# x given transposed as well, and phase A of a hybrid decoder layer in another order: two tiles ahead of their norm, the others normalised by spread factors

## The chip, the cores and the metric

One core of one Trainium2 chip runs the kernel. The metric is the device time of one execution in microseconds. TensorE is called PE, VectorE DVE, ScalarE ACT, GpSimd POOL and SyncE SP; SP and ACT issue the DMAs.

## The reference, cut to what matters

One decoder layer on 1024 prompt rows and 64 sample rows (8 sequences of 8), width 1024. Only the parts that the change touches are spelled out:

```
h    = x * rsqrt(mean(x*x) + EPS) * norm_g          # RMSNorm, row by row
proj = h @ w_in                                     # 1024 -> 3584: q, f, i, z_a, u, v, z_b, 512 columns each
o_a  = HGRN2 recurrence(silu(q), lb + (1-lb)*sigmoid(f), i)   # lb from a softmax of lb_logits
o_a  = rmsnorm_per_head(o_a, hgrn_norm_g) * silu(z_a)
v_n  = layernorm(gelu(v)) * ln_g + ln_b
o_b  = gelu(u) * (tril(w_s) @ v_n + b_s) * silu(z_b)          # per chunk of 128 rows and head
y    = rmsnorm(x + concat(o_a, o_b) @ w_out) * final_norm_g
```

Besides y the recurrent states and the last rows of v_n are put out. All inputs are float32.

## The kernel before, in words

Each large product is made of three: operand and weight are split into a high part (rounded to the fast float32 format of PE) and a low part (the rest), and high x high, low x high and high x low are accumulated in one bank of PSUM. A bank holds 128 x 512.

Rows are cut into nine tiles: 0 to 7 of the prompt, 128 rows each, and tile 8 with the 64 sample rows. The product needs x with the model's 1024 columns on the partitions, in eight slices of K of 128. `hT` holds that for all tiles, high and low.

The program runs in stages:

- Phase A, the I projection (`i`, 512 columns). Tile after tile: load the rows (`load_x`), square and sum them on ACT (`square_x`), mean and power of -0.5 on POOL (`rsqrt_mean`, L163), scale by that factor and by `norm_g`, which lies spread over all partitions in `gB` (`scale_x`, L202, DVE), eight transposes on PE into PSUM (`turn_x`, L210), the high part by ACT (`high_x`, L219), the low part by DVE (`low_x`, L223). Then `tm_part` (L261) issues 3 matmuls for each slice of K: 24 of 128x512 for a tile, 16 for tile 8, whose high and low parts stand side by side as one operand in `hs`. `evac_i` (L289) copies the bank to `vm`; for tile 8 two DMAs fold the two halves of the bank.
- Weights come by `load_wtm` (256 KB a slice), are rounded by ACT (`high_wtm`, L252) and their rest is taken by DVE or POOL (`low_wtm`, L256).
- Phase B, the V projection, does the same with the `v` columns on the finished `hT`, then GELU, layer norm and the spatial mix (`mix`). Three small setups run beside it; two of them use PE: a transpose of twelve rows of small vectors (L378), and four of `w_s` (L400).
- Then the five other column groups head by head (`et_part`, L497), interleaved with the recurrence, and last the output product (L1274) with the final norm.

PE's instructions stand in the order of the source in the whole program. The other engines follow a scheduler's order, apart from blocks under `manual_schedule`; in phase A that block covers tile 0 and part of tile 1 on DVE and ACT. SP issues its DMAs in order; a DMA into a buffer that is still read waits, and so do all behind it. `psm` has three banks for products, `psx` three for all else.

Of the kernel before, what the change touches and what calls it, by code (L numbers as in the profile page):

```python
# [90 lines left out]
def trunk(ctx, tc, x_prompt, x_sample, state, norm_g, w_in, lb_logits, hgrn_g, ln_g, ln_b, w_s, b_s, w_out,  # L91
          final_g, consts, y_prompt, y_sample, st_prompt, st_sample, vc_prompt, vc_sample):
# [75 lines left out]
    load_x(0)  # L168
    gB = px.tile([P, D], F32, name="gB")
    nc.sync.dma_start(gB, norm_g[0].partition_broadcast(P))  # L170
    nc.sync.dma_start(idt, consts[:, 0:P])

    warm = px.tile([P, 512], F32, tag="fb", name="warm")[:, :P]
# [10 lines left out]
    warm_up(12)  # L184

    def square_x(i):
        n = tiles[i][1]
        xt = xts[i]
        xn = px.tile([P, D], F32, tag="xn", bufs=2, name=f"xn{i}")
        ss = px.tile([P, 2], F32, tag="ss", bufs=2, name=f"ss{i}")  # L190
        if i == 0:
            for b, c in enumerate(HALVES):
                S.activation(xn[:, c], xt[:, c], AF.Square, accum_out=ss[:, b:b + 1])
            V.tensor_scalar(ss[:, 0:1], ss[:, 0:1], D * EPS, None, op0=ALU.add)
            V.tensor_scalar(ss[:, 0:1], ss[:, 0:1], ss[:, 1:2], 1.0 / D, op0=ALU.add, op1=ALU.mult)
            G.tensor_tensor(ss[:, 0:1], ss[:, 0:1], half_c[:, 0:1], op=ALU.pow)
        else:
            S.activation(xn[:n], xt[:n], AF.Square, accum_out=ss[:n, 0:1])
            rsqrt_mean(ss[:n, 0:1], ss[:n, 0:1], 1, D, n)
        xts[i] = (xt, xn, ss)  # L200

    def scale_x(i, b):  # L202
# [1 line left out]
        xt, xn, ss = xts[i]
        c = slice(512 * b, 512 * b + 512)
        V.scalar_tensor_tensor(xn[:n, c], xt[:n, c], ss[:n, 0:1], gB[:n, c], op0=ALU.mult, op1=ALU.mult)

    turned_x = {}

    def turn_x(i, b):  # L210
# [1 line left out]
        xn = xts[i][1]
        ps = bank(psx, f"xps{i}_{b}")
        pv = ps.rearrange("p (k t) -> p k t", k=4)
        for k in range(4):
            PE.transpose(pv[:, k, :n], xn[:n, (4 * b + k) * P:(4 * b + k + 1) * P], idt[:n, :n])
        turned_x[i, b] = pv[:, :, :n]
# [4 lines left out]

    def low_x(i, b):  # L223
        t0, n = tiles[i]
        hi, lo = (hT[:, j, 4 * b:4 * b + 4, t0:t0 + n] for j in range(2))
        V.tensor_tensor(lo, turned_x.pop((i, b)), hi.bitcast(F32), op=ALU.subtract)
# [1133 lines left out]
```

## Time and profile before

| | |
|---|---|
| median of three runs | 532.82 us (530.58 to 533.8) |
| profiled execution | 530.24 us, its span 528.1 us |
| mean granted clock of PE | 0.994 |
| first 128x512 matmul | 11.68 us |
| phase A ends, phase B begins | 70.40 us |
| time to landing of a 256 KB weight piece, median | 5.6 us |

Times in the rows are in microseconds from the start of the span. A row of the timeline has start, duration, engine, source line, operation, output and inputs, the shape, how many instructions are merged, and in brackets the idle time before it with what ended it. A matmul's duration includes its way through the array, so matmuls overlap, and the distance between two starts is what one costs. In a table by stretch each row has the stretch, its length, busy time of PE, PE's weight loads, DVE, ACT and POOL with their counts, the granted clock, the DMA engines' busy share and GB/s. Rows of groups have busy time and mean nanoseconds, then idle time before them.

### The profile page before, as it was taken

To read this page: it belongs to the slowest core of one execution; us is meant where nothing else is said; L and a number is where in the kernel's file an instruction comes from. 1 tells how busy PE (TensorE), PEld (TensorE's weight loads), DVE (VectorE), ACT (ScalarE), POOL (GpSimd) and SP (SyncE) were. 2 spreads that over 40 slices of the span, in tenths; PEclk is the share of its full clock that TensorE was granted. 3 is DMA by queue.
4 is the path that set the end of the run, shared out by engine and by line. 5 is a ranking of instruction groups with operands and counts; after the bars stand their busy time and mean duration, and the time that the engine had idled before them with its cause. 6 is when DMAs were issued, how large, how long until landed. Compare 5 with 4: busy or idle time off the path is not lost. (4 is left out here: it accounts for less than half of the span.)

```text
span 528.1 us, 10055 instructions
## 1 busy us (share of the span) xinstructions
PE 513.7 (97%) x3821; PEld 463.4 (88%) x3821; DVE 348.7 (66%) x1113; ACT 210.9 (40%) x568; POOL 68.5 (13%) x108
## 2 busy tenths in 40 slices
PE   7899999999999999999999999999998999999995
PEld 6677877889999999999999999999997968877884
DVE  3735266777499866886769866987847775445433
ACT  5545253211136435444436435444532163223321
POOL 1411046111001101000101001001120000100010
PEclk8999999999999999999999999999999999999998
DMA  8670144000002110111002110222234383223212
GB/s 283 208 238 22 36 96 123 17 0 1 20 22 60 44 41 6 47 56 42 21 28 60 41 42 6 81 68 72 79 89 123 99 271 131 96 107 94 92 72 76
DMA packets 41192, 41.06 MB, mean 78 GB/s; under 512 B 2220, under 2 KB 32440, under 8 KB 41144
## 3 DMA queue, kind: packets, MB, share of 16 engines
q1 hardware_dynamic: 40160, 39.36, 23.7%
q10 hardware_dynamic: 984, 1.06, 0.9%
q8 instruction: 30, 0.49, 0.4%
q14 instruction: 18, 0.15, 0.1%
HBM read 32.41 MB, written 7.21 MB: 75 GB/s over the span
## 5 line engine op out<-in xcount | busy, mean ns | idle before, releaser
L1274 PE MATMUL out<-wo,mhl 128*128 128x512 f32 (+2 forms) x306 | 70.5, 383 | 0.0
L1274 PEld LDWEIGHTS out<-wo,mhl 128*128 128x128 f32 (+1 forms) x306 | 54.5, 186 | 13.6 <-DVE wo L489 0.4
L497 PE MATMUL u<-hT,wehu 128*128 128x384 f32 (+1 forms) x192 | 47.9, 332 | 0.0
L497 PE MATMUL zb<-hT,wehzb 128*128 128x384 f32 (+1 forms) x192 | 47.8, 332 | 0.0
L497 PE MATMUL f<-hT,wehf 128*128 128x384 f32 (+1 forms) x192 | 47.7, 331 | 0.0
L497 PE MATMUL q<-hT,wehq 128*128 128x384 f32 (+1 forms) x192 | 47.7, 331 | 0.0
L497 PE MATMUL za<-hT,wehza 128*128 128x384 f32 (+1 forms) x192 | 47.4, 330 | 0.0
L272 PE MATMUL tmi<-wth,hT 128*128 128x512 f32 x128 | 41.4, 404 | 0.0
L272 PE MATMUL tm<-wth,hT 128*128 128x512 f32 x128 | 40.7, 398 | 0.0
L122 DVE TENSOR_TENSOR qv<-qv,fk 128x48 f32<-128x48 f32 (+4 forms) x132 | 38.7, 320 | 0.0
L497 PEld LDWEIGHTS za<-hT,wehza 128*128 128x128 f32 x192 | 33.5, 188 | 0.7 <-issue 0.2
L497 PEld LDWEIGHTS u<-hT,wehu 128*128 128x128 f32 x192 | 33.3, 188 | 0.6
L497 PEld LDWEIGHTS zb<-hT,wehzb 128*128 128x128 f32 x192 | 33.2, 188 | 0.6
L497 PEld LDWEIGHTS f<-hT,wehf 128*128 128x128 f32 x192 | 33.3, 188 | 0.4
L497 PEld LDWEIGHTS q<-hT,wehq 128*128 128x128 f32 x192 | 33.3, 188 | 0.0
L1286 DVE TENSOR_TENSOR r<-out,xr 128x512 f32<-128x512 f32 (+2 forms) x19 | 12.5, 660 | 30.6 <-PE out L1274 30.6
L497 PE MATMUL u<-hT,welu 128*128 128x384 f32 (+1 forms) x96 | 31.4, 327 | 0.0
L497 PE MATMUL zb<-hT,welzb 128*128 128x384 f32 (+1 forms) x96 | 31.4, 327 | 0.0
L497 PE MATMUL f<-hT,welf 128*128 128x384 f32 (+1 forms) x96 | 31.4, 327 | 0.0
L497 PE MATMUL za<-hT,welza 128*128 128x384 f32 (+1 forms) x96 | 31.4, 327 | 0.0
L497 PE MATMUL q<-hT,welq 128*128 128x384 f32 (+1 forms) x96 | 31.3, 326 | 0.0
L272 PE MATMUL tmi<-wtl,hT 128*128 128x512 f32 (+1 forms) x72 | 28.7, 399 | 0.0
(255 smaller groups left out, 1158.9 us busy)
## 6 DMA issues: line engine op xcount, KB each, us to landing
wst<-in_w_in SPq DMA_DIRECT2D x16, 256.0 KB, 5.6
wos<-in_w_out SPq DMA_DIRECT2D x16, 256.0 KB, 3.7
xr<-in_x_prompt SPq DMA_DIRECT2D x8, 512.0 KB, 3.4
xt<-in_x_prompt SPq DMA_DIRECT2D x7, 512.0 KB, 4.7
out<-r SPq DMA_DIRECT2D x7, 512.0 KB, 2.6
wesf<-in_w_in SPq DMA_DIRECT2D x8, 256.0 KB, 3.0
wesq<-in_w_in SPq DMA_DIRECT2D x8, 256.0 KB, 2.9
wesu<-in_w_in SPq DMA_DIRECT2D x8, 256.0 KB, 2.9
```

What stands on the lines that cost most here:

```text
L122: eng.tensor_tensor(o, a, b, op=ALU.mult)
L272: mmul(ps[:m], lhsT=a, rhs=w, start=(k == 0 and p == 0), stop=(k == 7 and p == len(pairs) - 1), skip_group_check=i == 8)
L497: mmul(ps[:, :b - a], lhsT=wt[:, k], rhs=hT[:, j, k, a:b], start=(k == 0 and p == 0), stop=(k == 7 and p == 2))
L1274: mmul(ps[:mm, :c.stop - c.start], lhsT=a, rhs=w[:, c], start=(k == korder[0] and p == 0), stop=(k == korder[-1] and p == len(pairs) - 1), ...
L1286: V.tensor_tensor(r[:n, c], ps[:n, :w], xr[:n, c], op=ALU.add)
```

## The change

- The host lays inputs out anew, without arithmetic: `xt_prompt` and `xt_sample` hold x transposed, `gcols` has `norm_g` as columns, `cols12` the small vectors as columns, `wst_s` has `w_s` transposed. So there are no transposes on PE any more (x, L216; the twelve rows, L378; `w_s`, L400), and no `gB`.
- Tiles 0 and 1 run ahead of their norm. Their transposed columns are multiplied by `norm_g` alone: the high part on ACT for tile 0 and on POOL for tile 1, the low part on DVE (`raw_high`, `raw_low`). Their matmuls go slice by slice, six for each slice of K, as the weights arrive. The factor of each row is applied at eviction (`scale=rms[i]`).
- The other tiles are normalised in columns (`norm_x`): POOL makes a diagonal matrix of the row factors (`diag_x`), PE multiplies a matrix of ones with it (`spread_x`, 128x128 in float32), which puts the factors of all rows on every partition, and DVE multiplies column slice, `norm_g` and spread factors, eight 128x128 steps a tile, then ACT and DVE split.
- Since `hT` must hold the normalised rows for the later products, tiles 0 and 1 are loaded and normalised a second time, beside tiles 3 to 6.
- The sample tile comes third instead of fifth. It is built in `hs`, and two DMAs copy it to `hT`.
- Rows are loaded besides columns, for the sum of squares only. Some loads go to parts of `vm` that are still free.
- Phase A has a fixed order on DVE, ACT and POOL, and for the first loads on SP and ACT.
- Phase B takes the tiles in the order 8, 2 to 7, 0, 1, and its setup has two parts.

The core of the diff:

```diff
@@ RAW tiles, loads
+    RAW = (0, 1)
+    def load_cols(i, k0=0, k1=KD, by=nc.sync, place=None):
...
+        by.dma_start(xcols[i][:, k0:k1, :n], (xt_prompt[i] if i < 8 else xt_sample)[:, k0:k1])
...
-    warm_up(12)
+    warm_up(10)
+    def raw_high(i, k, eng=None):
+        t0, n = tiles[i]
+        if eng:
+            eng.tensor_scalar(hT[:, 0, k, t0:t0 + n], col(i, k)[:, :n], gcol[:, k:k + 1], None, op0=ALU.mult)
+            return
+        S.activation(hT[:, 0, k, t0:t0 + n], col(i, k)[:, :n], AF.Copy, scale=gcol[:, k:k + 1])
+    def raw_low(i, k):
+        t0, n = tiles[i]
+        hi, lo = (hT[:, j, k, t0:t0 + n] for j in range(2))
+        V.scalar_tensor_tensor(lo, col(i, k)[:, :n], gcol[:, k:k + 1], hi.bitcast(F32), op0=ALU.mult, op1=ALU.subtract)
+    def rms_x(i):
+        n = tiles[i][1]
+        ss = px.tile([P, 1], F32, name=f"ss{i}")
+        x = xrows.pop(i)[:n]
+        S.activation(x, x, AF.Square, accum_out=ss[:n])
+        rsqrt_mean(ss[:n], ss[:n], 1, D, n)
+        rms[i] = ss
+        yield
+    def diag_x(i):
+        n = tiles[i][1]
+        dg = vm[:, 5 + len(spread) % 3, 7 * P:7 * P + n]
+        G.tensor_scalar(dg[:n], idt[:n, :n], rms[i][:n], None, op0=ALU.mult)
+        spread[i] = dg
+    def spread_x(i):
+        n = tiles[i][1]
+        ps = bank(psx, f"rb{i}")[:, :n]
+        mmul(ps, lhsT=ones[:n], rhs=spread[i][:n], start=True, stop=True)
+        spread[i] = ps
     def norm_x(i):
...
+        for b in range(2):
+            c = slice(4 * b, 4 * b + 4)
+            for k in range(4 * b, 4 * b + 4):
+                V.scalar_tensor_tensor(xn[:, k], col(i, k)[:, :n], gcol[:, k:k + 1], ps, op0=ALU.mult, op1=ALU.mult)
+                yield
+            S.activation(hi[:, c], xn[:, c], AF.Copy)
+        for b in range(2):
+            c = slice(4 * b, 4 * b + 4)
+            V.tensor_tensor(lo[:, c], xn[:, c], hi[:, c].bitcast(F32), op=ALU.subtract)
+            yield
+        if i == 8:
+            for j in range(2):
+                nc.sync.dma_start(hT[:, j, :, t0:t0 + n].bitcast(F32), hs[:, :, j].bitcast(F32))
...
     def evac_i(i, ps):
+        if i in RAW:
+            S.activation(vm[:, 0:4, i * P:i * P + P], ps.rearrange("p (h e) -> p h e", h=NH), AF.Copy, scale=rms[i])
...
+    seq = [8, 2, 3, 4, 5, 6, 7]
+        fetch_wtm(I_COL, s01, (0,))
+        load_cols(0, 0, 4)
+        load_cols(1, 0, 4, nc.scalar)
...
+        for k in range(KD):
+            if k == 0:
+                high_wtm(I_COL, k)
+            raw_high(0, k)
+            if k:
+                high_wtm(I_COL, k)
+            raw_high(1, k, G)
...
+            raw_low(0, k)
+            low_wtm(I_COL, k, V)
+            raw_low(1, k)
+            tm_part(ps0, I_COL, 0, (k,))
...
+            tm_part(ps1, I_COL, 1, (k,))
...
+        makes = {2: (4,), 3: (5,), 4: (6,), 5: (7,)}
+        diags = {2: (4, 0), 3: (5,), 4: (6, 1), 5: (7,)}
+        spreads = {2: (3,), 3: (4, 0), 4: (5,), 5: (6, 1), 6: (7,)}
...
+        for a, i in enumerate(seq):
+            ps = bank(psm, f"tmi{i}")
+            tm_part(ps, I_COL, i, range(2))
+            for j in spreads.get(i, ()):
+                spread_x(j)
+            tm_part(ps, I_COL, i, range(2, KD))
...
-        PE.transpose(ps[:, :12], rows, idt[:12, :12])
-        V.tensor_copy(col12, ps[:, :12])
...
-        for h in range(NH):
-            PE.transpose(pv[:, h], ws[:, h], idt)
-        S.activation(WT, pv, AF.Copy)
...
-    vseq = [0, 1, 8, 2, 3, 4, 5, 6, 7]
+    vseq = [8, 2, 3, 4, 5, 6, 7, 0, 1]
```

How the order moves, at the places where phase A is set. First PE at the start of the program, before (`xps` are the transposes, `tmi` the banks of the I product, `wth` and `wtl` the high and low weights by slice):

```order
L182 MATMUL warmup<-warm 128x128 x12
L216 MATMUL xps_0_171<-idt,xn_163 128x128 x4
L216 MATMUL xps_1_177<-idt,xn_163 128x128 x4
L182 MATMUL warmup<-warm 128x128 x4
L272 MATMUL tmi_160<-wth_0_125,hT 128x512 x2
L272 MATMUL tmi_160<-wtl_0_126,hT 128x512
L272 MATMUL tmi_160<-wth_1_129,hT 128x512 x2
```

and now:

```order
L208 MATMUL warmup<-warm 128x128 x10
L311 MATMUL tmi_177<-wth_0_118,hT 128x512 x2
L311 MATMUL tmi_177<-wtl_0_119,hT 128x512
L311 MATMUL tmi_178<-wth_0_118,hT 128x512 x2
L311 MATMUL tmi_178<-wtl_0_119,hT 128x512
L311 MATMUL tmi_177<-wth_1_120,hT 128x512 x2
L311 MATMUL tmi_177<-wtl_1_121,hT 128x512
L311 MATMUL tmi_178<-wth_1_120,hT 128x512 x2
L311 MATMUL tmi_178<-wtl_1_121,hT 128x512
```

The transposes of tile 0 and the four warm-up calls behind them are gone, and each slice of K now has the matmuls of tile 0 (`tmi_177`) and of tile 1 (`tmi_178`) before the next slice of weights is needed.

Next DVE at the start, before:

```order
L194 TENSOR_SCALAR ss_164<-ss_164 128x1
L195 TENSOR_SCALAR ss_164<-ss_164 128x1
L206 SCALAR_TENSOR_TENSOR xn_163<-xt_99,ss_164,gB 128x512 x2
L258 TENSOR_TENSOR wtl_0_126<-wst_0_123,wth_0_125 128x512
L226 TENSOR_TENSOR hT<-xps_0_171,hT 128x4x128
L258 TENSOR_TENSOR wtl_1_130<-wst_1_127,wth_1_129 128x512
L226 TENSOR_TENSOR hT<-xps_1_177,hT 128x4x128
L258 TENSOR_TENSOR wtl_2_134<-wst_2_131,wth_2_133 128x512
L258 TENSOR_TENSOR wtl_4_144<-wst_4_141,wth_4_143 128x512
```

and now (`xc_125` and `xc_127` are the columns of tiles 0 and 1):

```order
L222 SCALAR_TENSOR_TENSOR hT<-xc_125,gcol,hT 128x128
L297 TENSOR_TENSOR wtl_0_119<-wst_0_117,wth_0_118 128x512
L222 SCALAR_TENSOR_TENSOR hT<-xc_127,gcol,hT 128x128
L222 SCALAR_TENSOR_TENSOR hT<-xc_125,gcol,hT 128x128
L297 TENSOR_TENSOR wtl_1_121<-wst_0_117,wth_1_120 128x512
L222 SCALAR_TENSOR_TENSOR hT<-xc_127,gcol,hT 128x128
L222 SCALAR_TENSOR_TENSOR hT<-xc_125,gcol,hT 128x128
L297 TENSOR_TENSOR wtl_2_132<-wst_2_130,wth_2_131 128x512
L222 SCALAR_TENSOR_TENSOR hT<-xc_127,gcol,hT 128x128
```

The sums, the scaling of the rows and the reading of transposes from PSUM (`xps`) are gone. Each slice of K has two low parts of 128x128 and one low part of weights; all eight weight slices are DVE's, where POOL had three.

Last PE in the middle of a tile, before (tile 1):

```order
L272 MATMUL tmi_271<-wth_3_137,hT 128x512 x2
L272 MATMUL tmi_271<-wtl_3_138,hT 128x512
L216 MATMUL xps_0_284<-idt,xn_253 128x128 x4
L216 MATMUL xps_1_291<-idt,xn_253 128x128 x4
L272 MATMUL tmi_271<-wth_4_143,hT 128x512 x2
L272 MATMUL tmi_271<-wtl_4_144,hT 128x512
```

and now (tile 3, `rb` are the spread factors):

```order
L311 MATMUL tmi_408<-wth_1_120,hT 128x512 x2
L311 MATMUL tmi_408<-wtl_1_121,hT 128x512
L253 MATMUL rb_415<-vm 128x128
L253 MATMUL rb_417<-vm 128x128
L311 MATMUL tmi_408<-wth_2_131,hT 128x512 x2
L311 MATMUL tmi_408<-wtl_2_132,hT 128x512
```

In place of eight transposes for the next tile stands one product with the matrix of ones, or two where a tile is normalised for the second time.

More of the change, by code (lines that the diff above doesn't have):

```diff
@@ L166, in rsqrt_mean @@
         G.tensor_tensor(out, out, half_c[:rows, :n_cols], op=ALU.pow)
[L168 to L173, printed above, removed]
+    gcol = keep.tile([P, KD], F32, name="gcol")
+    nc.scalar.dma_start(gcol, gcols)
+    warm = px.tile([P, D], F32, tag="xs", bufs=2, name="warm")[:, :P]
     V.memset(warm, 0.0)
@@ L202, in scale_x @@
-    def scale_x(i, b):
-        n = tiles[i][1]
[L204 to L210, printed above, removed]
-        n = tiles[i][1]
[L212 to L217, printed above, removed]
@@ new lines, in trunk, with load_wtm, fetch_wtm @@
+    wparts = {}
+    def load_wtm(col, ks, place):
+        st = place[0].tile([P, KD, P], F32, tag=place[1], name=f"wst{col}_{ks[0]}").rearrange("p k e -> p (k e)").rearrange(
+            "p (j c) -> p j c", j=2)
+        for k in ks:
+            hi = wtm.tile([P, 512], F32R, tag="wth", name=f"wth{col}_{k}")
+            lo = wtm.tile([P, 512], F32R, tag="wtl", name=f"wtl{col}_{k}")
+            wparts[col, k] = (hi, lo, st[:, k % 2])
+        return st
+    def fetch_wtm(col, st, ks, by=nc.sync):
+        src = win[ks[0] * P:(ks[-1] + 1) * P, col:col + 512].rearrange("(j p) c -> p j c", p=P)
+        by.dma_start(st[:, ks[0] % 2:ks[0] % 2 + len(ks)], src)
@@ L342, in trunk @@
[L342 to L357 removed]
+            t = px.tile([P, 2, 512], F32, tag="xs", bufs=2, name="ifold")
@@ new lines, in evac_i @@
+            folded(t[:, 0], t[:, 1], ps)
+            fold.append(lambda: V.tensor_tensor(vis, t[:, 0], t[:, 1], op=ALU.add))
+    seq = [8, 2, 3, 4, 5, 6, 7]
+    places = [(we, "weh")] * 3 + [(we, "wel")] * 3
+    s01 = load_wtm(I_COL, (0, 1), places[0])
+    with tc.manual_schedule(engines={mybir.EngineType.Activation, mybir.EngineType.SP}):
+        fetch_wtm(I_COL, s01, (0,))
+        load_cols(0, 0, 4)
+        load_cols(1, 0, 4, nc.scalar)
+        fetch_wtm(I_COL, s01, (1,))
+        fetch_wtm(I_COL, load_wtm(I_COL, (2, 3), places[1]), (2, 3))
+        load_cols(0, 4, KD)
+        load_cols(1, 4, KD)
+        S.activation(lb, half_c[:, 0:NH], AF.Sigmoid)
+        load_rows(8)
+        fetch_wtm(I_COL, load_wtm(I_COL, (4, 5), places[2]), (4, 5))
+        nc.sync.dma_start(idt, consts[:, 0:P])
+        xcols[8] = px.tile([P, KD, P], F32, tag="xs", bufs=2, name="xc8")
+        load_cols(8)
+        fetch_wtm(I_COL, load_wtm(I_COL, (6, 7), places[3]), (6, 7))
+        load_rows(2)
+        load_cols(2)
+        load_rows(0, place=2)
+        load_rows(3)
+        load_cols(3, place=1)
+        load_rows(1, place=3)
+        nc.sync.dma_start(cst, consts[:, P:])
+        nc.sync.dma_start(col12, cols12)
+        load_rows(4)
+        load_cols(4, place=2)
@@ L417, in evac_v @@
         if i == 8:
-            fa, fb = folded(pv_, ps, "vfold", ("fa", 1, "fb", 1))
+            fa, fb = (pv_.tile([P, 512], F32, name=f"vfold{j}") for j in range(2))
+            folded(fa, fb, ps)
             src = fb[:n]
```

251 lines of the change are left out of this document (116 added, 135 removed).

## The prediction

> **What bounds the kernel now.** I read the page's table of engines first, then a table of busy time by stretch, then PE's own timeline through phase A (the I projection), where the change works.
>
> ```profile
> PE 513.7 (97%) x3821; PEld 463.4 (88%) x3821; DVE 348.7 (66%) x1113; ACT 210.9 (40%) x568; POOL 68.5 (13%) x108
> ...
> 0.00:11.60 11.60, 8.26 (x39) 7.78 (x40) 4.12 (x11) 5.69 (x12) 0.76 (x5) 0.92 0.78 268
> 11.60:70.40 58.80, 56.74 (x276) 45.51 (x274) 30.13 (x43) 29.84 (x57) 12.28 (x21) 0.99 0.41 129
> 70.40:130.00 59.60, 59.60 (x288) 48.67 (x287) 42.60 (x82) 15.96 (x28) 17.28 (x24) 1.00 0.17 47
> 130.00:528.10 398.10, 389.10 (x3224) 361.49 (x3222) 271.83 (x979) 159.37 (x474) 38.17 (x59) 1.00 0.22 69
> ```
>
> PE is busy from end to end: this is a chain of matmuls, and time is saved only by removing work from PE, or by starting it sooner. DVE has about half its time free between 11.6 and 70.4, ACT too. Next, what PE does there:
>
> ```profile
> 1.04 5.45 PE L182 MATMUL warmup<-warm 128*128 128x128 f32 x24 [1.04 <-DVE euler L176]
> 8.78 1.54 PE L216 MATMUL xps<-idt,xn 128*128 128x128 f32 x8 [2.29 <-DVE xn L206]
> ...
> 11.68 1.20 PE L272 MATMUL tmi<-wth,hT 128*128 128x512 f32 x2
> ...
> 15.70 0.40 PE L272 MATMUL tmi<-wtl,hT 128*128 128x512 f32 x1
> 17.06 0.66 PE L216 MATMUL xps<-idt,xn 128*128 128x128 f32 x4 [0.96 <-DVE xn L206]
> 18.82 0.63 PE L216 MATMUL xps<-idt,xn 128*128 128x128 f32 x4 [1.10 <-DVE xn L206]
> 19.20 0.72 PE L272 MATMUL tmi<-wth,hT 128*128 128x512 f32 x2
> ...
> 23.96 0.39 PE L272 MATMUL tmi<-wtl,hT 128*128 128x512 f32 x1
> 24.20 1.03 PE L216 MATMUL xps<-idt,xn 128*128 128x128 f32 x8
> 24.99 0.72 PE L272 MATMUL tmi<-wth,hT 128*128 128x512 f32 x2
> ...
> 70.17 0.39 PE L272 MATMUL tmi<-wtl,hT 128*128 128x512 f32 x1
> 70.40 0.63 PE L272 MATMUL tm<-wth,hT 128*128 128x512 f32 x2
> ```
>
> From 70.17 to 70.40 one 128x512 matmul takes 0.233 us: a tile of 128 rows (24 matmuls) takes 5.6 us, the sample tile (16) takes 3.73. All nine are 48.5 us, but phase A ends at 70.40. The rest is: no matmul before 11.68; a stall of tile 0 from 15.94 to 19.20 behind the transposes of tile 1; and eight transposes in each later tile, 0.79 us from 24.20 to 24.99.
>
> As a check of this accounting: 19.20 to 70.40 is 51.2 us. Nine matmuls of tile 0 (2.1), seven tiles (39.2), the sample tile (3.7) and seven sets of transposes (six of 0.79, about 0.7 for the sample's) make 50.4. The 0.8 left over, 0.1 a tile, I carry into the sum for after.
>
> **The change part by part.** *Removed from PE:* all 72 transposes of x, and in phase B two small sets:
>
> ```profile
> 75.77 0.40 PE L272 MATMUL tm<-wtl,hT 128*128 128x512 f32 x1
> 76.09 0.23 PE L378 MATMUL ps<-idt,rows 12*128 12x12 f32 x1
> 76.25 0.74 PE L272 MATMUL tm<-wth,hT 128*128 128x512 f32 x2
> ...
> 81.73 0.39 PE L272 MATMUL tm<-wtl,hT 128*128 128x512 f32 x1
> 81.96 0.60 PE L400 MATMUL psw<-idt,ws 128*128 128x128 f32 x4
> 82.32 0.48 PE L272 MATMUL tm<-wth,hs 128*128 128x512 f32 x1
> ```
>
> From 75.77 to 76.25 is 0.48, less one matmul of 0.233: 0.25 us. From 81.73 to 82.32 is 0.59, less one: 0.36. Phase B saves 0.6.
>
> *Added on PE:* nine float32 products with the matrix of ones, 128x128. The nearest rows are four float32 mixes of that size (two records each):
>
> ```profile
> 92.03 1.16 PE L451 MATMUL mix<-WT,vg 128*128 128x128 f32 x8
> 92.94 0.72 PE L272 MATMUL tm<-wth,hT 128*128 128x512 f32 x2
> ```
>
> 0.91 us for four: 0.23 each. Two fall before the sample tile, seven after it: 1.6 us.
>
> *The start.* The first matmul no longer waits for a norm, a scaling and a transpose. It needs a 256 KB piece of weights, half of tile 0's columns, and a conversion on ACT. The rows that price this:
>
> ```profile
> 3.42 0.63 ACT L193 ACTIVATE xn<-xt 128x512 f32<-128x512 f32 x1 [1.19 <-DMA xt<-in_x_prompt]
> ...
> L254 ACT ACTIVATE wth<-wst x8: 615/624/632, 8.8 to 14.8; 128x512 fp32r<-128x512 f32 x8
> L898 ACT ACTIVATE on<-o,oss 128x128 f32<-128x128 f32 x32 | 9.6, 366 | 7.7 <-POOL oss L166 7.7
> ```
>
> Today's first load, of the same 256 KB, has landed at 3.42, the second about 1.1 later. So weights are at hand at 3.4, columns at 4.5 (up to 5.3, since a third load shares the engines), and 0.62 and 0.37 of ACT give the first operands at 4.9 to 5.7. The warm-up is ten calls instead of twelve: 1.04 + 5.45 x 10/12 = 5.6. First matmul at 5.6 instead of 11.68.
>
> From there six matmuls a slice of K, 1.4 us, are 11.2 us, if fed. The last weights decide. Ahead of them and with them 3.74 MB stand in the queue (weights 2.10, columns 1.05, sample 0.52, identity 0.07); today the same 3.74 MB (weights 2.10, x0 and x1 1.05, the spread gain 0.52, identity 0.07) have landed when the last conversion starts at 14.8. So slice 6 begins near 14.3, is converted by 14.9, and then DVE has two slices left. DVE's rows:
>
> ```profile
> 404.95 2.15 DVE L1072 SCALAR_TENSOR_TENSOR s<-s,s_a,s_u 128x128 f32<-128x128 f32 x8
> 25.51 1.28 DVE L226 TENSOR_TENSOR hT<-xps,hT 128x512 fp32r<-128x512 f32 x2
> 24.18 1.42 DVE L206 SCALAR_TENSOR_TENSOR xn<-xt,ss,gB 128x512 f32<-128x512 f32 x2 [1.83 <-POOL ss L166]
> 15.24 3.43 DVE L206 SCALAR_TENSOR_TENSOR xn<-xt,ss,gB 128x512 f32<-128x512 f32 x2 [0.72 <-POOL ss L166]
> ```
>
> Eight 128x128 scalar_tensor_tensor in 2.15 are 0.26 apart; 128x512 subtractions come 0.6 apart. A slice is 2 x 0.26 + 0.61 = 1.13 on DVE, under PE's 1.4, plus four 128x64 steps of the sample's norm (0.21 each, an estimate from the 0.26) after slices 5 and 6. From 14.9: 0.61 + 0.26 + 0.84 + 1.13 = 17.75, and PE finishes at 18.0.
>
> The last row holds the cost that I can't place exactly. The same pair of operations takes 3.43 us at 15.24 and 1.42 at 24.18. Beside the first one GpSimd was at work:
>
> ```profile
> 13.83 0.75 POOL L165 TENSOR_SCALAR ss<-ss 128x1 f32<-128x1 f32 x1
> 15.18 2.95 POOL L258 TENSOR_TENSOR wtl<-wst,wth 128x512 fp32r<-128x512 f32 x2
> 19.47 0.19 POOL L165 TENSOR_SCALAR ss<-ss 128x1 f32<-128x1 f32 x1 [1.35 <-ACT xn L198]
> L122 POOL TENSOR_TENSOR qm<-s_q,cst 128x128 f32<-128x128 f32 x8 | 3.5, 474 | 2.5 <-PE s_sc L1056 1.8 <-ACT s_q L943 0.7
> ```
>
> The two engines keep each other out. The change gives GpSimd eight scalings of 128x128 (tile 1's high parts), in two bursts of four, in the very stretch where DVE subtracts. One costs between 0.19 (128x1, alone) and 0.47 (128x128 with two inputs); I take 0.33, the middle, 2.65 us in all. The first burst falls where DVE waits for weights, the second where it doesn't: 1.3 us. The sample tile then starts at 18.0 + 1.3 + 0.23 = 19.5. Bounds: 17.3 (5.6 + 11.2 + two products of 0.23) and 22.0 (18.0 + 8 x 0.47 + 0.23).
>
> *The steady part.* A norm is now eight 128x128 steps and two subtractions on DVE, 8 x 0.26 + 2 x 0.61 = 3.3 us. Tiles 0 and 1 are normalised a second time, beside tiles 3 to 6. Eight norms of 3.3 are 26 us under 35 us of PE, and the fullest tile carries 3.3 + 1.0 + 1.2 = 5.5 of 5.8. I cost it at nothing; what it costs if that cover goes is a rival below. ACT has two halves of 0.6, a square of 1.25 and an eviction of 0.6 a tile: 3.1 of 5.8.
>
> *The loads.* x comes twice (rows for the norm, columns for the product), and tiles 0 and 1 have their columns loaded again. Tile 4's columns must be in near 30.7; 8.3 MB stand up to them.
>
> ```profile
> 10.00:12.50 2.50, 2.50 (x12) 2.40 (x11) 2.50 (x5) 2.49 (x6) 0.31 (x1) 0.50 1.04 393
> 12.50:15.00 2.50, 2.50 (x10) 1.95 (x10) 0.78 (x2) 2.50 (x6) 2.33 (x3) 0.87 1.04 401
> ...
> 20.00:22.50 2.50, 2.50 (x12) 2.04 (x11) 2.01 (x3) 0.98 (x3) 0.30 (x1) 1.00 0.97 244
> ```
>
> Today 11.6 x 268 plus 3.4 x about 397 make 4.46 MB by 15.0. The other 3.83 MB take 9.8 us at 390 GB/s (in at 24.8), 15.7 at 244 (30.7, just in time). SP issues in order and stands behind ACT's eviction of the sample tile (its fold) before it asks for the last rows and columns; that is near 29, with 12 us to go before tile 6 needs them.
>
> *The sum.* Phase A ends at 19.5 + 3.73 + 6 x 5.6 + 1.6 + 0.8 = 59.2 instead of 70.40: 11.2, with phase B's 0.6 it is 11.8. Behind that nothing is moved. The span goes from 528.1 to 516.3. The profiled execution took 530.24, under the three runs shown (median 532.82); what lies around the span stays. I set the saving against the median: 532.8 - 11.8 = **521.0**.
>
> [...] The row at 10.00 shows a granted clock of 0.50, and 0.87 behind it, after a hole of only 2.3 us (6.5 to 8.78): 2.5 x 0.50 + 2.5 x 0.13 = 1.6 us of PE lost. After the change PE is fed piece by piece from 5.6 on, with holes that I put under 1.5 us, and I take no loss. [...]
>
> **The rivals.**
>
> *A crawling start (0.18).* GpSimd's scalings at 0.47 each, all visible on DVE (2.5 over my start), and one clock drop (1.6): 521.0 + 4.1 = 525.1. For it: the 3.43 row and the 0.50. Against: DVE waits for weights in the first half anyway. [...]
>
> *Loads late (0.09).* Up to and with the V weights 15.4 MB must land (the 8.3 above, 4.2 for tiles 5 to 7 and the two reloads, 0.8 of copies of the sample tile, 2.1 of weights); 4.46 are in by 15.0, and 10.9 remain. At 244 GB/s they take 45 us, to 60, which is about when they are used. At half of today's 390, as short pieces (1 KB and 256 bytes) might make it, they take 56, to 71: the whole head start is gone, about 531. Against: at 390 it is 28 us, to 43.
>
> *DVE becomes the bound (0.05).* If the 128x128 step that reads the spread factors from PSUM cost far more than 0.26, the norms would set the pace: eight of 8s + 1.21 against 35.2 us. From s = 0.39 they decide; from 0.57 the change loses. At 0.75, what the 128x512 step costs, they are 57.7: 22.5 more, 532.8 - 11.8 + 22.5 = 543.5. Against: the row with 0.26 also reads PSUM.
>
> **How the numbers follow.** The forecast has 0.68. The best start (17.3) gives 518.8, and a run's scatter of 1 us or so 517.5; the crawling start 525.1, with scatter 526.0. The range 517.5 to 526.0 holds both, less their tails, about 0.8. A measurement tells about 1%, 5.3 us: faster 0.86 (forecast and crawl), same 0.09, slower 0.05.
>
> **What would show it.** First 128x512 matmul near 5.6; the sample tile's near 19.5; phase B's first near 59; DVE's 128x128 steps 0.26 apart; no idle time of PE between tiles. I am wrong if DVE's steps come 0.4 apart, if PE waits for loads after 25 us, or if stages behind phase B grow.

## The result, and the profile after

The change takes the median from 532.73 us (530.58 to 533.8, four runs) to **518.96 us** (518.77 to 519.61, four runs): a ratio of 0.9749 with a 95% interval of 0.9717 to 0.978. 521.0 was predicted, 517.5 to 526.0 as the range. The total is close, but one large term was wrong, and others made up for it. The profiled execution took 519.07, its span 517.3.

| us | before | before, profiled again | after | predicted |
|---|---|---|---|---|
| first 128x512 product | 11.68 | 12.27 | 5.80 | 5.6 |
| start of the sample tile (end of the two-tile start) | - | - | 24.02 | 19.5 |
| phase B begins | 70.40 | 72.44 | 63.06 | 59.2 |
| length of phase B, to the first product of `f` | 55.38 | 55.38 | 54.37 | 54.8 |
| `f` to the first product of `z_a` | 233.38 | 233.38 | 233.45 | 233.4 |
| `z_a` to the first output product | 63.29 | 65.18 | 61.63 | 63.3 |
| output product to the end | 105.65 | 105.92 | 104.79 | 105.65 |

PE's timeline after, in the columns known from before:

```profile
5.80 0.90 PE L311 MATMUL tmi<-wth,hT 128*128 128x512 f32 x2 [0.47 <-ACT hT L217]
...
11.89 0.40 PE L311 MATMUL tmi<-wtl,hT 128*128 128x512 f32 x1
14.36 0.73 PE L311 MATMUL tmi<-wth,hT 128*128 128x512 f32 x2 [2.08 <-ACT wth L293]
...
23.88 0.39 PE L253 MATMUL rb<-vm 128*128 128x128 f32 x2
24.02 0.48 PE L311 MATMUL tmi<-wth,hs 128*128 128x512 f32 x1
...
63.06 0.40 PE L311 MATMUL tm<-wth,hs 128*128 128x512 f32 x1
```

The start ran to 12.1 with one gap of 0.19 us, then PE waited 2.08 us for the conversion of the fifth slice of weights (k = 4). From 24.02 on there is no idle time up to phase B. The table by stretch, same columns as before (granted clock, DMA share and GB/s last):

```profile
7.50:10.00 2.50, 2.50 (x12) 2.03 (x11) 2.37 (x7) 1.45 (x3) 1.60 (x2) 1.00 1.08 257
10.00:12.50 2.50, 2.28 (x10) 1.50 (x8) 0.84 (x2) 0.15 (x1) 0.00 (x0) 1.00 1.04 226
12.50:15.00 2.50, 0.64 (x2) 0.30 (x2) 1.02 (x2) 2.50 (x6) 1.24 (x3) 1.00 1.16 317
15.00:17.50 2.50, 2.50 (x7) 1.67 (x7) 1.57 (x4) 1.04 (x3) 2.50 (x5) 0.51 1.03 407
17.50:20.00 2.50, 2.50 (x7) 1.93 (x6) 2.50 (x10) 1.08 (x3) 0.71 (x1) 0.50 1.06 373
20.00:22.50 2.50, 2.50 (x9) 1.98 (x8) 2.50 (x10) 2.50 (x7) 1.15 (x2) 0.62 1.07 356
```

Two things stand out. Between 7.5 and 12.5 us the DMA engines are busy throughout (share above 1) and move only 257 and 226 GB/s, where they move 356 to 407 later. And behind the hole the clock is 0.51, 0.50 and 0.62: of 7.5 us, 3.4 are lost. What the other engines did then:

```profile
12.35 1.06 ACT L236 ACTIVATE xt<-xt 64x1024 f32<-64x1024 f32 x1 [2.80 <-DMA xt<-in_x_sample]
15.32 2.88 POOL L215 TENSOR_SCALAR hT<-xc,gcol 128x128 fp32r<-128x128 f32 x4
15.96 1.18 DVE L222 SCALAR_TENSOR_TENSOR hT<-xc,gcol,hT 128x128 fp32r<-128x128 f32 x2 [0.93 <-POOL hT L215]
16.30 0.63 ACT L293 ACTIVATE wth<-wst 128x512 fp32r<-128x512 f32 x1 [0.89 <-DMA wst<-in_w_in]
...
21.83 0.75 DVE L269 TENSOR_TENSOR hs<-xn,hs 128x256 fp32r<-128x256 f32 x2
L215 POOL TENSOR_SCALAR hT<-xc,gcol x8: 593/688/1181, 5.8 to 17.1; 128x128 fp32r<-128x128 f32 x8
```

ACT stood 2.80 us in front of the square of the sample's rows (tile 8), which had not landed; the conversions for k = 4 stand behind it. POOL makes the factors and the diagonal from that square, and only then tile 1's scalings of k = 4 to 7, 0.69 us each (last row: minimum, median and maximum in ns). DVE waits for the first of them, and then works without a gap from 15.96 to 22.6. The weights of k = 6 were in only at 16.30. From this I had three suspects for the lost 4.5 us: small pieces that slow the loads, ACT in order behind the rows, and the clock.

### The profile page after: what moved, and what is told of

Its sections match the earlier page's. It is cut to its first block, busy times and chain, and to the rows that moved or that the text cites. A ratio compares the mean times of both kernels' runs of the same rounds, so it can differ in the third digit from the quotient of the medians.

```text
span 517.3 us, 10015 instructions
## 1 busy us (share of the span) xinstructions
PE 506.2 (98%) x3750; PEld 456.6 (88%) x3750; DVE 359.8 (70%) x1184; ACT 211.7 (41%) x569; POOL 78.6 (15%) x123
## 5 line engine op out<-in xcount | busy, mean ns | idle before, releaser
L311 PE MATMUL tmi<-wth,hT 128*128 128x512 f32 x128 | 43.0, 418 | 2.5 <-ACT wth L293 2.1
L311 PEld LDWEIGHTS tmi<-wth,hT 128*128 128x128 f32 x128 | 24.7, 198 | 9.3 <-ACT wth L293 2.5
L1359 DVE TENSOR_TENSOR r<-out,xr 128x512 f32<-128x512 f32 (+2 forms) x19 | 12.5, 660 | 29.2 <-PE out L1347 29.2
```

Of the source, the lines that this page charges most:

```text
L311: mmul(ps[:m], lhsT=a, rhs=w, start=(k == 0 and p == 0), stop=(k == 7 and p == len(pairs) - 1), skip_group_check=i == 8)
L1359: V.tensor_tensor(r[:n, c], ps[:n, :w], xr[:n, c], op=ALU.add)
```

## The experiments

Each kernel but the repeat of before is the changed kernel with the edit shown; experiment 10 takes over the edit of 9, and 11 that of 10. A measured time is the median of its executions; in brackets stand its ratio to the kernel before and the 95% interval of the ratio. "Start" is the start of the sample tile, 24.02 after the change. Lines left out of an edit are marked with three dots.

**1. The sample's transposed x packed.**

```diff
-        xcols[8] = px.tile([P, KD, P], F32, tag="xs", bufs=2, name="xc8")
+        xc8 = px.tile([P, KD, P], F32, tag="xs", bufs=2, name="xc8")
+        xcols[8] = xc8.rearrange("p k t -> p (k t)")[:, :KD * NS].rearrange("p (k t) -> p k t", k=KD)
```

> The sample tile's transposed x is stored packed, so its 256 KB load goes in rows of 2 KB instead of pieces of 256 B; nothing else changes. Small pieces (theory): they are what lowered the rate to 226 to 257 GB/s in 7.5 to 12.5 us at a full DMA share, so the rows of tile 8 land about 1.5 us sooner (12.35 now), the hole before the weight part k = 4 shrinks from 2.1 to 0.6 us or less, the clock is not lowered, and the sample tile starts at 19.5 to 20.5 instead of 24.0: 3.5 to 4.5 us less in all. Bytes alone (rival): the same bytes stand ahead of the same loads, so the hole stays at about 2 us, the start at 24, and the time within 0.3 us. Shut gate alone (second rival: the clock would be lowered whatever the hole): the hole shrinks but the clock row still shows 0.5, and the gain is 1.5 us at most.

Measured: 519.25 us (0.9754, 0.9737 to 0.9771), start 23.89. The packets under 512 bytes between 5 and 15 us fell from 1164 to 143, and the rate between 7.5 and 12.5 us was still 281 and 220 GB/s. The small pieces of the sample's columns are not the cause. The hole was gone, because PE came to it later (first product at 6.52, clock 0.51 between 7.5 and 10), and that gained nothing.

**2. The square of the sample's rows one slice later.**

```diff
-            if k == 3:
+            if k == 4:
                 list(rms_x(8))
                 diag_x(8)
```

(and `spread_x(8)` at k = 5 instead of 4.)

> ScalarE's square over the sample's rows stands one weight part later (behind the conversion of k = 4 instead of k = 3), with its diagonal and its spread; the loads are untouched. In-order wait (theory): ScalarE stood behind the late rows of tile 8, not behind weights, so the conversion of k = 4 moves from 13.69 to when its weights land; if they landed by 12, the hole goes from 2.1 to 0.5 us or less and the sample tile starts at 20 to 21, 3 to 4 us less. Late transfers (rival): the weights of k = 4 land as late as the rows, the hole stays above 1.5 us, and the time moves by less than 0.7 us.

Measured: 519.2 us (0.975, 0.9731 to 0.9768), start 23.77: the rival. ACT, now free to take the weights first, waits for them just as long:

```profile
13.11 0.63 ACT L293 ACTIVATE wth<-wst 128x512 fp32r<-128x512 f32 x1 [3.15 <-DMA wst<-in_w_in]
```

The weights of k = 4 land only at 13.1. They stand behind the rows in the same queue (after the change the rows are asked for at 4.07 us, these weights at 4.67), and both are late.

**3. TensorE kept busy through the hole.**

```diff
+            if k == 4:
+                warm_up(8)
             tm_part(ps0, I_COL, 0, (k,))
```

> Eight extra 128x128 products of zeros into the unused warm-up bank stand on TensorE ahead of the weight part k = 4, that is in the hole of 2.1 us; no load and no other engine changes. Clock (theory): the hole is what lowers the granted clock to 0.5 from 15 to 22 us, and it cost about 3.4 us; with TensorE busy through the hole the clock rows stay at 1.00, the hole itself stays (k = 4 still begins near 14.4), and the sample tile starts at about 20.5, 3 to 3.5 us less. No gate (rival): the clock falls anyway, or the feed of k = 5 to 7 (weights converted at 14.5, 16.3, 19.5) sets the pace in its place: the gain is under 1.5 us.

Measured: 519.03 us (0.9748, 0.9733 to 0.9763), start 23.34. The clock did stay up, and the start came 0.7 us sooner. But the sample's rows landed 0.7 us sooner in this run as well (ACT's square begins at 11.64 instead of 12.35), so nothing is left that the clock must have given: the rival. The table by stretch, then ACT, DVE and PE of this run:

```profile
15.00:17.50 2.50, 2.50 (x10) 1.46 (x10) 2.24 (x5) 0.63 (x1) 2.50 (x4) 1.00 1.02 396
17.50:20.00 2.50, 2.39 (x10) 1.48 (x9) 2.50 (x11) 1.76 (x4) 0.03 (x1) 1.00 1.06 376
```

```profile
11.64 1.06 ACT L236 ACTIVATE xt<-xt 64x1024 f32<-64x1024 f32 x1 [2.25 <-DMA xt<-in_x_sample]
15.26 1.20 DVE L222 SCALAR_TENSOR_TENSOR hT<-xc,gcol,hT 128x128 fp32r<-128x128 f32 x2 [0.93 <-POOL hT L215]
...
21.15 0.75 DVE L269 TENSOR_TENSOR hs<-xn,hs 128x256 fp32r<-128x256 f32 x2
23.10 0.49 PE L253 MATMUL rb<-vm 128*128 128x128 f32 x2 [0.88 <-POOL vm L246]
```

Here is the long link: DVE has 6.6 us of work without a gap from 15.26 to 21.9 (seven low parts of x, three of weights, eight steps of the sample's norm and its two subtractions), and PE follows piece by piece. Then PE waits 0.88 us for the diagonal of tile 2, whose spread stands ahead of the sample tile; POOL makes it behind ACT's square of tile 2, which stands in ACT's list behind work that waits for DVE. The same wait ends the start in experiments 1, 2, 5, 6 and 8 (0.70 to 0.89 us). After the change, at half clock, PE had no gap in that stretch and came to the spread at 23.88, when the diagonal had been done since 23.72: two limits of about equal length, of which taking one away shows nothing.

**4. Tile 1's scalings on ScalarE.**

```diff
-            raw_high(1, k, G)
+            raw_high(1, k)
```

> Tile 1's eight raw scalings in the start are ScalarE's (as tile 0's are) instead of GpSimd's; nothing else changes. Theory (a chain from the late rows of tile 8: square on ScalarE, factor and diagonal on GpSimd, then GpSimd's raw scalings of k = 4 to 7, then VectorE's list, which runs without a gap from about 15.3 to 21.9 in the runs with a full clock): one link goes, VectorE's wait of 0.93 us for GpSimd ends, and the first tile after the two starts 0.5 to 1 us sooner, if ScalarE's eight more scalings (0.3 each behind one another) don't eat it. Rival (late weights decide): the weights of k = 6 and 7 land at about 15.5 whatever GpSimd does, the start is where it was, within 0.3 us of 23.9, and so is the time.

Measured: 519.17 us (0.9735, 0.9678 to 0.9793), start 23.57, no gain that can be told. But the rows landed later in this run, and behind them the chain is shorter:

```profile
13.26 1.06 ACT L236 ACTIVATE xt<-xt 64x1024 f32<-64x1024 f32 x1 [1.58 <-DMA xt<-in_x_sample]
```

From the square's begin to the start are 10.3 us here. After the change they are 11.7 (12.35 to 24.02), in experiment 1 as well (12.19 to 23.89) and in experiment 3 (11.64 to 23.34), with quite different clocks. That the distance stays the same while its ends move by 0.7 us is the best evidence for the chain, and it is 1.4 us shorter without POOL's scalings. This is one profile, and PE, at half clock for part of the time (0.994 in the mean of this run), had no gap from 15.27 on; the end of DVE's work, which stands before PE, came 1.6 us nearer to the square (8.6 us behind its begin, 10.2 after the change).

**5. The sample's rows asked for sooner.** `load_rows(8)` and the identity stand right behind the weights of k = 2 and 3.

```diff
         fetch_wtm(I_COL, load_wtm(I_COL, (2, 3), places[1]), (2, 3))
+        load_rows(8)
+        nc.sync.dma_start(idt, consts[:, 0:P])
         load_cols(0, 4, KD)
         load_cols(1, 4, KD)
...
-        load_rows(8)
...
-        nc.sync.dma_start(idt, consts[:, 0:P])
```

> The sample's rows (and the identity) are asked for right behind the weights of k = 2 and 3, ahead of the second halves of tile 0's and 1's transposed x, so 0.5 MB sooner in the queue; bytes and engines' lists are the same. Theory (the chain that begins at the late rows): the rows land 1 to 1.5 us sooner than 12.2, GpSimd's diagonal and its scalings of k = 4 to 7 follow, VectorE's unbroken stretch begins 0.5 to 1 us sooner, and the sample tile starts at 22.8 to 23.3: 0.5 to 1.2 us less in all. Rival (weights of k = 4 to 7 landing at about 13.1 and 15.5 decide): the start stays within 0.3 us of 23.9. It also shows whether the stretch of 115 to 230 GB/s between 8.5 and 11.5 us moves to an earlier time with these rows (a transfer into 64 partitions only) or stays where it is.

Measured: 518.35 us (0.973, 0.9684 to 0.9777), start 22.90, phase B at 61.93. The first experiment in which the start moves as the chain from the rows says, by 1.1 us, although the first product came late in this run (7.19):

```profile
10.05 0.63 ACT L293 ACTIVATE wth<-wst 128x512 fp32r<-128x512 f32 x1 [1.61 <-DMA wst<-in_w_in]
11.40 1.04 ACT L236 ACTIVATE xt<-xt 64x1024 f32<-64x1024 f32 x1
22.90 0.48 PE L311 MATMUL tmi<-wth,hs 128*128 128x512 f32 x1
```

From the square to the start are 11.5 us. ACT now waits for weights ahead of the square and no longer for the rows themselves. In the whole time the interval doesn't tell it from the change. The slow stretch moved too: 198 GB/s between 7.5 and 10 us, 347 between 10 and 12.5. It goes where the sample's rows go.

**6. The sample's rows over all partitions.** What is special about them: 64 rows fill 64 partitions. This kernel leaves half of each row out of the sample's sums.

```diff
+        if i == 8:
+            nc.sync.dma_start(xrows[i][:, :512], src.rearrange("t (c d) -> (t c) d", c=2))
+            return
         nc.sync.dma_start(xrows[i][:n], src)
...
+        m = n if i < 8 else P
+        x = xrows.pop(i)[:m] if i < 8 else xrows.pop(i)[:, :512]
```

> The changed kernel with the sample's rows loaded as 128 half rows of 2 KB into 128 partitions instead of 64 rows of 4 KB into 64; the sample's factors are then computed from wrong sums (half a row), so this part of the result is left out, and ScalarE's square is 0.4 us shorter. Theory (a transfer into 64 partitions only is what holds the rate at 115 to 230 GB/s between 8.5 and 11.3 us): the stretch goes, the windows of 7.5 to 12.5 us show 330 GB/s or more instead of 257 and 226, the rows land 1 to 1.5 us sooner and so do the weights behind them (k = 6's conversion at 14.5 to 15 instead of 15.5 to 16.3). Rival (the rate is low there for another reason, such as the source of the second halves of the transposed x): the stretch stays, with rates within 10% of 257 and 226.

Measured (one execution): 517.6 us, span 515.8; start 21.55, phase B at 60.59, 2.5 us sooner than after the change. The stretch and ACT:

```profile
7.50:10.00 2.50, 2.48 (x6) 2.00 (x7) 2.50 (x7) 1.57 (x4) 2.50 (x3) 0.50 1.06 404
10.00:12.50 2.50, 2.50 (x11) 2.00 (x10) 1.77 (x6) 1.81 (x5) 1.47 (x4) 0.82 1.17 301
```

```profile
10.29 0.63 ACT L240 ACTIVATE xt<-xt 128x512 f32<-128x512 f32 x1 [0.59 <-DMA xt<-in_x_sample]
14.44 0.63 ACT L297 ACTIVATE wth<-wst 128x512 fp32r<-128x512 f32 x1 [0.99 <-DMA wst<-in_w_in]
```

404 GB/s instead of 257 (and 301 instead of 226, where 330 or more was expected), the rows 2.1 us sooner, the weights of k = 6 at 14.4 instead of 16.3. The same 256 KB into 64 partitions held up all that stood behind it. The edit also halves the pieces, from 4 KB to 2 KB, and no run takes the two apart. Against the length of the pieces speaks the profile after the change: the rows of tile 2, pieces of 4 KB too but for 128 partitions, were asked for at 8.3 us and landed 9.2 us later, at the end of the stretch with 407 GB/s. The stretches of 2.5 us hold other loads too; from 8.5 to 11.5 us after the change 162 GB/s were moved at a full share (1.04). Why a load into 64 partitions should be slower is shown by no run. From the square to the start are 11.3 us, 11.7 less the 0.4 by which the square is shorter: the same chain, begun sooner. The clock was 0.50 between 7.5 and 10 us, which cost nothing that shows. Of the 2.5 us the span shows 1.5 (515.8 against 517.3): the stretch from the output product to the end took 105.60 here and 104.79 after the change.

**7. The two tiles taken apart**, to price the idea of the start: tile 1's products all behind tile 0's.

```diff
-            tm_part(ps1, I_COL, 1, (k,))
             if k == 7:
+                tm_part(ps1, I_COL, 1, range(KD))
                 spread_x(2)
```

> The two-tile start taken apart: in the start TensorE does only tile 0's products with each weight part as it comes; tile 1's 24 products stand behind tile 0's last ones. Loads and the other engines' lists are the same (the sample's spread stays behind k = 4). Theory (the start is set by a chain on the other engines that ends at about 22 us, and TensorE fills its waits with tile 1): tile 1's 24 products (0.234 us each, 5.6 us) now stand behind that end, apart from the 0.7 to 0.9 us that TensorE waits there anyway: the sample tile starts at 27 to 29 us instead of 24.0 and the time is 3.5 to 5 us longer. Rival (TensorE sets the pace of the start): the same products in another order cost nothing, within 0.5 us.

Measured: 524.15 us (0.9849, 0.9831 to 0.9868), 5.2 us over the change (the profiled execution 4.1):

```profile
14.15 0.74 PE L311 MATMUL tmi<-wth,hT 128*128 128x512 f32 x2 [2.72 <-ACT wth L293]
...
28.07 0.48 PE L311 MATMUL tmi<-wth,hs 128*128 128x512 f32 x1
```

The start ends 4.05 us later. So of the 5.6 us of tile 1's products in the start some 4 lay in waits of PE, at much the same clock (0.67, 0.50 and 0.50 here in the stretches from 15 to 22.5 us, 0.51, 0.50 and 0.62 after the change).

**8. Transposes put back**, eight of the identity behind each spread of tiles 3 to 7, 0 and 1.

```diff
+        if i not in (8, 2):
+            jk = bank(pss, f"jk{i}")
+            for h in range(8):
+                PE.transpose(jk[:, h % 4 * P:h % 4 * P + P], idt, idt)
```

> Eight transposes of the 128x128 identity into an unused bank stand behind each spread of tiles 3 to 7, 0 and 1: 56 of the kind that the change took off TensorE (eight took 0.79 us before), with no reader. Theory (TensorE sets the pace in the steady part): phase B starts 7 x 0.79 = 5.5 us later, and the time is 5 to 5.8 us longer. Rival (TensorE waits there for VectorE's and ScalarE's normalisation anyway, so the transposes were covered): under 1 us.

Measured: 525.91 us (0.9875, 0.9826 to 0.9924), 6.95 over the change, more than the 5 to 5.8 expected:

```profile
23.50 0.48 PE L315 MATMUL tmi<-wth,hs 128*128 128x512 f32 x1
...
29.10 1.04 PE L258 MATMUL jk<-idt 128*128 128x128 f32 x8
...
68.76 0.40 PE L315 MATMUL tm<-wth,hs 128*128 128x512 f32 x1
```

From the start to phase B are 45.26 us instead of 39.04: 6.2 for seven sets, 0.89 each. (The start came 0.5 us sooner, and 1.3 us of the rest lie behind phase B.) The steady part was PE's, and each set of transposes cost its full time there.

**9. All links at once.** Rows early as in 5; raw scalings and low parts of k = 4 to 7 ahead of the late weights; the sample's norm in one piece; tile 2's square and spread inside the sample tile.

```diff
+            if k == 3:
+                list(rms_x(8))
+                diag_x(8)
+                for j in (4, 5):
+                    raw_high(0, j)
+                    raw_high(1, j)
+                    raw_low(0, j)
+                    raw_low(1, j)
...
             if k == 5:
-                norm8 = norm_x(8)
...
+                list(norm_x(8))
```

> All links of the start's chain at once: rows of tile 8 early as in the run with early rows; the raw scalings and their low parts for k = 4 to 7 ahead of the late weights' conversions, in VectorE's hole of 2 us (six of the eight highs on ScalarE, two on GpSimd behind the diagonal); the sample's normalisation in one piece between the weights of k = 5 and 6, so ScalarE does not stand before it; tile 2's square, diagonal and spread behind the start, inside the sample tile. Theory: VectorE has 6.7 us of work from about 12.2, so the sample tile starts at 19 to 20.5 instead of 24, 3.5 to 5 us less, and the time is 514 to 515.5. Rival (the weights of k = 6 and 7, landed at 15.5, are the wall): TensorE still has twelve products of k = 6 and 7 and the rest of k = 5 behind them, and with conversions the start is not below 19; if they land later still, the gain is under 2 us. Second rival: tile 2 is then late and gives 1 us or more back before it.

Measured: 519.59 us (0.9754, 0.97 to 0.9808). The start is 2.5 us sooner, not the 3.5 to 5 expected, and tile 2 (27.89 after the change) gives 1.5 of it back, the second rival:

```profile
21.50 0.39 PE L311 MATMUL tmi<-wth,hs 128*128 128x512 f32 x1
...
26.89 0.50 PE L311 MATMUL tmi<-wth,hT 128*128 128x512 f32 x1 [1.30 <-ACT vm L329]
```

**10. The same, mended at its waits.**

```diff
-    ps0, ps1 = bank(psm, "tmi0"), bank(psm, "tmi1")
+    ps0, ps1 = bank(psm, "tmi0"), bank(pss, "tmi1")
...
+            if k == 6:
+                high_wtm(I_COL, 6)
+                high_wtm(I_COL, 7)
```

> The run with all links at once, mended at its three new waits: the sample's spread ahead of k = 4's products instead of between them, both conversions of k = 6 and 7 ahead of ScalarE's copies of the normalised sample, and tile 1's sums in a bank that is otherwise empty here, so tile 2 does not wait for tile 0's eviction (1.30 us in that run). Theory (the start's end is the end of a chain of links, each of which is the next to decide): the sample tile starts at 19.8 to 20.8, tile 2 follows it without the 1.3 us of wait, phase B starts at 59.5 to 60.8 instead of 62.3 to 63.1, and the time is 516 to 517: 2 to 3 us less than the changed kernel. Rival (what is saved ahead of the sample tile is given back at tile 2 and 3, whose rows come later than TensorE then wants them): phase B still starts at 62 or later and the time is within 1 us of 519.

Measured: 518.97 us (0.9754, 0.9733 to 0.9774). Start at 20.12 and tile 2 at 24.04, as the theory said; phase B at 62.10, as the rival said:

```profile
20.12 0.39 PE L311 MATMUL tmi<-wth,hs 128*128 128x512 f32 x1
...
24.04 0.40 PE L311 MATMUL tmi<-wth,hT 128*128 128x512 f32 x1
36.55 1.06 ACT L236 ACTIVATE xt<-xt 128x1024 f32<-128x1024 f32 x1 [5.85 <-DMA xt<-in_x_prompt]
38.27 0.49 PE L311 MATMUL tmi<-wth,hT 128*128 128x512 f32 x1 [1.54 <-ACT hT L266]
```

Of the 3.9 us gained at the start 2.9 are lost before phase B, some 2.2 of them at tile 4 and 0.5 at tile 2: ACT stands 5.85 us before the rows of tile 5, and the copies of tile 4, which PE wants, stand behind it in ACT's order. These rows did not come sooner with the start: they were asked for at 30.72 (30.43 after the change) and landed 5.8 us later in both. After the change ACT stood before them too, for 3.10 us up to 36.22, which PE did not feel. The transfers run at a full share (1.00 to 1.08 in all stretches of 5 us from 20 to 40), and each tile now needs x twice; that this is what keeps the request back was not tested.

**11. With wide rows and the copies ahead of the squares.** Besides, the halves of the sample's rows are added by the spread, its transposed x is packed as in 1, and rows are asked for one tile sooner.

```diff
+            V.tensor_scalar(rb, ps, EPS, None, op0=ALU.add)
+            G.tensor_tensor(rb, rb, half_c[:, 0:1].to_broadcast([P, NS]), op=ALU.pow)
...
+            if new:
+                list(norm_x(new[0]))
             for j in makes.get(i, ()):
                 list(rms_x(j))
...
-            if new:
-                list(norm_x(new[0]))
```

> The version that the runs point to: the mended start, and the three things that still held it. The sample's rows come as 128 half rows into all partitions (as in the run with wide rows) with the right sums: the halves are added by the spread itself through a 128x64 matrix of pairs, and the power is taken on the 128x64 result, one GpSimd operation that no earlier trace shows on this shape. The sample's transposed x is packed. In the steady part ScalarE copies the tile that TensorE wants next before it squares the rows of the tile after it, and those rows are asked for ahead of tile 0's second load. Theory (after the start, phase A is paced by transfers at a full DMA share until about 50 us, and by ScalarE standing in order behind late rows): the sample tile starts at 18.5 to 19.8 us, no tile behind it waits over 0.5 us, phase B starts at 58.8 to 60.3 instead of 62 to 63, and the time is 515 to 516.5: 2.5 to 4 us less than the changed kernel. Rival (the transfers alone decide: 10 MB in phase A end when they end): phase B starts at 60.5 to 61.5 and the time is 517 to 518. Second rival: the power on 128x64 takes 3 us or more, the sample's columns wait for it, and the start is back at 22 or later.

Measured: 529.84 us (0.995, 0.9927 to 0.9972): the second rival, and far beyond it.

```profile
13.01 10.94 POOL L272 TENSOR_TENSOR rb<-rb,half_c 128x64 f32<-128x64 f32 x1 [0.95 <-DVE rb L271]
26.45 0.80 PE L333 MATMUL tmi<-wtl,hT 128*128 128x512 f32 x1 [9.83 <-DVE wtl L319]
```

The wide rows did their part, this time with whole rows in the sums:

```profile
7.50:10.00 2.50, 2.50 (x12) 2.06 (x11) 2.45 (x7) 2.04 (x5) 1.83 (x3) 1.00 1.05 398
10.00:12.50 2.50, 2.50 (x13) 2.05 (x11) 2.50 (x10) 2.50 (x10) 0.73 (x1) 1.00 1.06 391
```

But the power on 128x64 took 10.94 us; on 128x1 it takes 0.57. From these two shapes I estimate 0.16 us for each further column, so the factors should be made before they are spread. A version with whole sums made before the spread wasn't tried, so no run here is a finished kernel that beats the change by more than the measurement can tell.

**12. The kernel before, profiled again.**

> The kernel before, unchanged, profiled once more. If the 1.7 us that the change gained between z's last part and the output stage (wait for the state's load 1.9 us before, 0.3 after) is chance in the landing of a store, this profile shows a wait other than 1.9 us, or one as long as before with the same landings; if it belongs to the kernel, the wait is 1.7 to 2.1 again. The stretch from output to end (105.7 before, 104.8 after) likewise: 105.5 to 105.9 if it is the kernel's. The span should lie between 528 and 531.

Measured: 534.44 us, span 532.3, over the expected range. PE's wait for the state's load was 2.33 us, 1.90 in the first profile and 0.28 after the change. The rows of before again, then of after:

```profile
411.72 2.14 PE L1056 MATMUL s_sc<-s,qm 128*32 128x128 f32 x30 [2.33 <-DMA s<-in_state_hgrn]
...
411.00:417.00 6.00, 5.28 (x43) 4.61 (x44) 1.96 (x7) 0.00 (x0) 0.00 (x0) 0.72 0.27 82
...
out<-s SPq DMA_DIRECT2D x8, 256.0 KB, 3.5
```

```profile
399.34 1.28 PE L1131 MATMUL s_sc<-s,qm 128*32 128x128 f32 x30 [0.28 <-DMA s<-in_state_hgrn]
...
out<-s SPq DMA_DIRECT2D x8, 256.0 KB, 2.4
```

The wait is outside the 1.7 to 2.1 us that were to show a property of the kernel, so this run alone does not settle it. But in all twelve profiles of the changed kernel and its variants the wait is 0.3 to 0.7 us, and in both of before 1.9 or more, so I take it for a property of the program and not for chance. The load waits on SP for an earlier store of the state to land (last rows: issues, size, median us to landing), and that takes 3.5 us in both profiles of before, 2.4 after. Why the same store lands sooner in the changed program was not tested and stays open. In this run the hole of 2.33 us was followed by a clock of 0.72; behind the 1.90 of the first profile the clock stayed at 1.00. That accounts for 1.5 us of the difference between the two profiles of before.

## Why the prediction was right, and where it was wrong

**The first product, 5.6: right.** 5.80; over the twelve kernels it is 5.8 to 7.2, set by when the first columns land.

**The start, 19.5 with bounds of 17.3 and 22.0: wrong, 24.02.** The step that failed is "the last weights decide", with DVE's two last slices behind them from 14.9. The weights of k = 6 came 2.0 us later (16.3 instead of 14.3), and DVE then had more than two slices left: from 15.96 it worked 6.6 us without a gap. GpSimd's scalings were undersized one by one, 0.69 us instead of 0.33 and above my upper bound of 0.47, but experiment 4 puts them at some 1.4 us of the path, where the sum had 1.3; they are not where the 4.5 us went. What the sum lacked was the chain that starts at the sample's rows: 256 KB into 64 partitions, at 257 and 226 GB/s between 7.5 and 12.5 us, hold up the rows and all weights behind them; ACT's square, POOL's diagonal and POOL's scalings come in order behind that; DVE's 6.6 us follow, and behind DVE come PE and the diagonal of tile 2, which the sum left out as well. I had set 3.74 MB after against 3.74 MB before; the bytes are the same, but before, these rows stood far behind the first weights. Experiment 6 mends it at its head: 2.5 us, in one execution.

The rival of the crawling start put this point at 19.5 + 4.1 = 23.6, the nearest number of all, by scalings at 0.47 and one clock drop. The scalings were dearer and the drop came, but the number is near by luck: experiment 4 leaves the scalings near what the forecast had, and in experiment 3, with the clock at 1.00, the start came no sooner than its rows, where the clock rows show 3.4 us as lost. A half clock on an engine that waits for its feed cost little here.

**The steady part: right in its numbers, wrong in one reason.** From the start to phase B it is 39.04 against my 39.7; the spreads took about 0.15 instead of 0.23, the DVE steps came 0.26 to 0.27 apart, and no idle time of PE stands between the tiles. Experiment 8 shows that PE sets the pace there. The loads were priced by tile 4's columns, "in at 24.8 to 30.7, just in time". What I did not price are the rows of tile 5: ACT stands in order before them, and tile 4's copies stand behind them. After the change that was covered only because the start was late; with the start at 20.12, experiment 10 waits at tile 4, and phase B begins at 62.10. With the order of that kernel my 19.5 and my 59.2 do not go together. In experiment 6, from 21.55, PE had no wait there.

**Phase B: right in kind**, 1.0 us saved instead of 0.6; where the other 0.4 came from was not looked for.

**"Behind that nothing is moved": wrong by 2.5 us in the span.** The stretch from `z_a` to the output saved 1.66, the stretch from the output to the end 0.86. The first is the wait for the state's load (experiment 12), a property of the programs whose cause is open. The second varies from 104.7 to 105.7 in the variants, and 105.65 and 105.92 in the two profiles of before; I can't place it.

**How the sum came out.** Against the forecast span of 516.3: phase A 3.9 later, phase B 0.4 less, the two last stretches 2.5 less, 517.3. The spans of the two profiles differ by 10.8 us, the medians by 13.8. The profiled execution of before was a quick one: of 38 other runs of that kernel, with spans of 527.0 to 532.9 us, three were quicker. "What lies around the span stays" therefore failed: the forecast laid 4.7 us on its span (532.8 less 528.1), and after the change the median lies 1.7 above the span of the profile, 3 us less. With the 2.9 us of the later stages that makes 6 us too much, against 4 too little at the start. The forecast was good to 2 us because these two errors point opposite ways, which is luck.

## What to carry to other kernels

Price a start by the chain of last arrivals through each engine's list, not by bytes and by the work of one engine; an operation that waits for a late load holds up all that stands behind it on its engine (ACT stood 2.80 us in front of the sample's rows, with the conversions of k = 4 behind them, and 5.85 us in front of tile 5's in experiment 10). When two limits are of about equal length, taking one away shows nothing, so three edits without effect do not clear the three suspects; the link that feeds both (here one load into half of the partitions) has to be found. A stage that is just in time behind a late start may not be so behind an early one: move the start, and look for the next load.
